# Layer norms given out in small steps, their stores issued from POOL, and the last sums shared by two engines, in a two-layer float32 encoder

## The chip, the cores and the metric

The kernel runs on one core of one Trainium2 chip. The metric is the time of one execution in microseconds on the device; three runs are compared by their median. A profile of one execution shows each engine (PE is TensorE, DVE VectorE, ACT ScalarE, POOL GpSimd, SP SyncE, whose queue issues most DMAs), instruction by instruction. PEclk is the share of its full clock that TensorE was granted.

## The reference

An encoder trunk of two layers runs over two token streams, one of 1024 and one of 256 tokens, each with 16 learned tokens put in front (1040 and 272 positions of 1024 channels, float32). Cut to what matters here:

```python
for i in range(2):
    m = hyena_mixer(h, ...) if i == 0 else attention_mixer(h, ...)
    h = layer_norm(ALPHA * h + m, ln1_g[i], ln1_b[i])
    g, a = jnp.split(h @ ffn_w_in[i], 2, axis=-1)        # 2 x 2816 channels
    f = (gelu(dwconv3(g, conv_w, conv_b)) * a) @ ffn_w_out[i]
    h = layer_norm(ALPHA * h + f, ln2_g[i], ln2_b[i])
return h[:, 16:]

def layer_norm(x, g, b):
    xc = x - mean(x, channels)
    return xc * rsqrt(mean(xc * xc, channels) + 1e-5) * g + b
```

The change is in the second layer norm of each layer, the one behind the product with `ffn_w_out`.

## The kernel before

**Layout.** Channels lie on the 128 partitions in 8 blocks, tokens along the free axis. The tokens of both streams are put into two pairs of chunks: pair p = 0 has two chunks of 384 tokens, pair p = 1 has two of n1 tokens (272 in layer 0; 258 in layer 1, where 14 positions that are not returned are left out). The two chunks of a pair are called c = 0 and c = 1.

**Products.** Each float32 operand is split into a rounded part and a remainder: a cast by ACT (line 259) and a subtraction by DVE (line 260). Each product is three matmuls (lines 288 to 290).

**`ffn_out`** (line 1009) computes the product with `ffn_w_out`. It works in two halves: c = 0 holds the first half of the tokens (chunk 0 of both pairs, up to 656 columns, kept in 8 tiles C), c = 1 the second. Within a half it goes through groups of channel blocks: two groups of four blocks for c = 0; three groups, of 3, 3 and 2 blocks, for c = 1. In a group it goes through the 22 blocks of the inner dimension. Each such step loads a piece of the weight (`raw`, line 1022) and a piece of the hidden values (`hraw`, line 1026) by SP's queue and splits both (`w`, `hq`); up to three steps are prepared ahead (list `ready`), with 4 buffers for `raw`, 3 for `hraw` and 8 each for `w` and `hq` (two to a step). The first two and the last two steps of a group go together (`cuts`). At the last one the residual is loaded into C (line 1054), and DVE adds the product out of PSUM (line 1062) and sums the channel blocks per token into `sms` (line 769).

**The norms as background work.** When a half is done, its two norms (p = 0 and p = 1) are put into a list of generators, `bg`. Each yields the time, in microseconds, after which its next piece is due. After each channel block `ffn_out` calls

```python
                        self.tick(0.9 * (k1 - k0))
```

which takes that time off each generator's count and issues the next piece of those that are due. So the norms of c = 0 are issued between the products of c = 1. Those of c = 1 are issued between the next layer's query, key and value products (layer 0), or at the end by `drain`, which steps the generators in turn, the last one first (layer 1).

**`layer_norm`** (line 771) has these pieces: the mean by a matmul with a constant matrix (line 781); for each of 8 blocks, in two pieces of four, a subtraction (DVE, line 786), a square (ACT, line 788), and the addition of the square into `sm` (POOL, line 790); then the variance by small matmuls (line 796) and the reciprocal root (lines 820 to 825, on ACT and DVE in turn); then the spread of it over the partitions by matmuls (line 804), and for each block, again four and four, a scaling (DVE, line 809), an addition of the bias (ACT, line 810) and `done(f)`. The first matmuls of the mean, the variance and the spread are kept in program order on TensorE. All other instructions are ordered by a scheduler at build time, engine by engine, by program order and its own estimate of when each could run.

**`done`** is `to_x` in layer 0: it splits the block into the operands `y` for the next products and stores it to the buffer `x2d` (line 1403). In layer 1 it is `to_y`, which stores the block to the output (line 1411). Both store by SP's queue, the queue that also loads `raw` and `hraw`. PSUM's tag `ln` (2 banks) holds the mean, the variance and the spread of both norms. The tiles `tp` (9 buffers) hold sums and squares.

`layer_norm` is also used by `window_norms`, for the first norm of each layer.

Of the kernel before, what the change touches and what calls it, by code (L numbers as in the profile page):

```python
# [12 lines left out]
ALU = mybir.AluOpType  # L13
# [65 lines left out]
LAYERS = (Layout(0, 272), Layout(T0, 258))  # L79
# [168 lines left out]
class Trunk:  # L248
# [519 lines left out]
        if f:  # L768
            self.nc.vector.tensor_tensor(out=sm, in0=A[0] if f == 1 else sm, in1=A[f], op=ALU.add)

    def layer_norm(self, A, sm, idx, done):


        nc = self.nc
        v = nc.vector
        n = sm.shape[-1]
        b = self.lnp[:, idx + 1]
        ps = lambda: self.pps.tile([128, 512], F32, tag="ln", name=self.n("ln"), bufs=2)[:, :n]
        mu = ps()
        pin = self.tc.keep_in_program_order  # L780
        pin(nc.tensor.matmul(out=mu, lhsT=self.o1024, rhs=sm, start=True, stop=True))
        nb = -(-n // 128)
        m = 2 * -(-n // (2 * nb))
        at = [min(m * i, n - m) for i in range(nb)]
        for f in range(KC):
            v.tensor_tensor(out=A[f], in0=A[f], in1=mu, op=ALU.subtract)
            sq = sm if f == 0 else self.tp(n)
            nc.scalar.activation(out=sq, in_=A[f], func=AF.Square)  # L788
            if f:
                nc.gpsimd.tensor_tensor(out=sm, in0=sm, in1=sq, op=ALU.add)  # L790
            if f == 3:
                yield 1.5
        yield 8
        var = ps()
        for i, o in enumerate(at):
            x = nc.tensor.matmul(out=var[:m, i:i + 1], lhsT=sm[:, o:o + m], rhs=self.o1024[:, 0:1], start=True, stop=True)
            if i == 0:
                pin(x)
        small = lambda: self.tmp.tile([128, 4], F32, tag="rs", name=self.n("rs"), bufs=6)[:m, :nb]
        r = self.rsqrt(small, var[:m, :nb], nb, self.eps[:m, 0:1], LN_EPS)  # L800
        yield 1.5
        rb = ps()
        for i, o in enumerate(at):
            x = nc.tensor.matmul(out=rb[:, o:o + m], lhsT=r[:, i:i + 1].to_broadcast([m, 128]), rhs=self.ident[:m, :m],
                                 start=True, stop=True)
            if i == 0:
                pin(x)
        for f in range(KC):
            v.scalar_tensor_tensor(out=A[f], in0=A[f], scalar=self.lng2[:, idx, f:f + 1], in1=rb, op0=ALU.mult, op1=ALU.mult)
            nc.scalar.activation(out=A[f], in_=A[f], func=AF.Identity, bias=b[:, f:f + 1])  # L810
            done(f)
            if f == 3:
                yield 3

    def rsqrt(self, t, var, n, eps, epsv, out=None):
# [193 lines left out]
    def ffn_out(self, l, idx, done):  # L1009


        nc = self.nc
        v = nc.vector
        lay, w = LAYERS[l], self.a["w_fout"][l]
        N2 = lay.N2
        half = 2 * -(-N2 // 4)
        sides = ((0, half), (half, N2))

        def load(c, m0, m1, kp):
            cols = (m1 - m0) * 128  # L1020
            r = self.wk.tile([128, 512], F32, tag="raw", name=self.n("raw"), bufs=4)[:, :cols]
            nc.sync.dma_start(out=r, in_=w[kp, :, m0 * 128:m1 * 128])
            wh, wl = (self.wk.tile([128, 512], F32R, tag="w", name=self.n("w"), bufs=8)[:, :cols] for _ in range(2))
            self.split(r, wh, wl)
            r = self.dn.tile([128, 656], F32, tag="hraw", name=self.n("hraw"), bufs=3)[:, :N2]
            nc.sync.dma_start(out=r, in_=self.hd[l][c, kp, :, :N2])
            hh, hl = (self.dn.tile([128, 656], F32R, tag="hq", name=self.n("hq"), bufs=8)[:, :N2] for _ in range(2))
            self.split(r, hh, hl)
            return wh, wl, hh, hl

        groups = ([(0, 0, 4), (0, 4, 8)], [(1, 0, 3), (1, 3, 6), (1, 6, 8)])
        steps = [(*g, kp) for c in range(2) for g in groups[c] for kp in range(MF)]
        cuts = (0, 2) + tuple(range(3, MF - 1)) + (MF,)
        ready = []

        def unit():
            while len(ready) < 3 and steps:
                ready.append(load(*steps.pop(0)))
            return ready.pop(0)

        for c in range(2):
            C = [(self.dn, self.cb)[c].tile([128, 656], F32, tag="c", name=self.n("C"), bufs=8) for _ in range(KC)]
            sms = [self.tp(n) for n in lay.n]
            for _, m0, m1 in groups[c]:
                ps = {}
                for k0, k1 in zip(cuts, cuts[1:]):
                    us = [unit() for _ in range(k0, k1)]
                    for m in range(m0, m1):
                        q = slice(128 * (m - m0), 128 * (m - m0) + 128)
                        A = C[m]  # L1050
                        if k1 == MF:
                            for p in range(2):
                                o = lay.start[p][c]
                                nc.sync.dma_start(out=A[:, 384 * p:384 * p + lay.n[p]], in_=self.xd[l][:, m, o:o + lay.n[p]])
                        for i, (a, b) in enumerate(sides):
                            if k0 == 0:
                                tag, bufs = ("mm", 6) if m - m0 < 3 else ("ln", 2)
                                ps[m, i] = self.pps.tile([128, 512], F32, tag=tag, name=self.n("mm"), bufs=bufs)[:, :b - a]
                            self.mm3(ps[m, i], [(wh[:, q], wl[:, q], hh[:, a:b], hl[:, a:b]) for wh, wl, hh, hl in us],
                                     k0 == 0, k1 == MF)  # L1060
                            if k1 == MF:
                                v.scalar_tensor_tensor(out=A[:, a:b], in0=A[:, a:b], scalar=ALPHA, in1=ps[m, i],
                                                       op0=ALU.mult, op1=ALU.add)
                        if k1 == MF:
                            for p in range(2):
                                self.add_up(sms[p], [z[:, 384 * p:384 * p + lay.n[p]] for z in C], m)
                        self.tick(0.9 * (k1 - k0))
            for p in range(2):
                A = [z[:, 384 * p:384 * p + lay.n[p]] for z in C]
                self.later(("x", 2 * p + c), self.layer_norm(A, sms[p], idx, done(p, c, A)))  # L1070


    def qkv(self, common, later):
# [320 lines left out]
        o = lay.start[p][c] - 1 + d[p and c]  # L1394
        return x[:, m, o:o + lay.n[p] + 2]

    def to_x(self, p, c, A):
        lay = LAYERS[0]
        o, n, at = lay.start[p][c], lay.n[p], c * lay.n[p]

        def f(k):
            self.split(A[k], self.x[p][0][k][:, at:at + n], self.x[p][1][k][:, at:at + n])
            self.nc.sync.dma_start(out=self.x2d[:, k, o:o + n], in_=A[k])
        return f

    def to_y(self, p, c, A):
        s = p and c
        o = LAYERS[1].start[p][c] - LAYERS[1].col(s, T0)

        def f(k):  # L1410
            self.nc.sync.dma_start(out=self.a[f"y_{s}"][:, k, o:o + LAYERS[1].n[p]], in_=A[k])
        return f


# [18 lines left out]
```

## Time and profile before

| | |
|---|---|
| median of 3 runs | 3626.16 us (3624.95 to 3626.39) |
| profiled execution, its time | 3623.7 us |
| span of the profile | 3621.5 us |
| mean granted clock of TensorE | 0.973 |
| DMA moved | 391.69 MB, 108 GB/s |
| DMAs issued by POOL (software queue) | 23.07 MB |

The page of the profile names groups of instructions by line, engine and tile, with their count, busy time and the idle time before them. A view by windows gives the busy time of each engine in a stretch of the execution, with the number of instructions in brackets, the granted clock, the mean busy share of the 16 DMA engines and what they moved. A timeline row gives start, duration, engine, line, operation, tiles, shapes and count, and in square brackets how long the engine was idle before and what it waited for. A row may merge instructions of one line; the shape shown is that of the first.

### The profile page before, as it was taken

Reading aid. Unit: us, or ns where it says so; the run is one execution under the profiler, and the core shown is the slowest. Engines: PE = TensorE matmul, PEld = TensorE weight load, DVE = VectorE, ACT = ScalarE, POOL = GpSimd, SP = SyncE. Lnnn points to the kernel's source line nnn. Section 1 sums busy time; section 2 is a strip of 40 time slices with the busy share of each in tenths; the row PEclk is TensorE's granted clock in tenths of the full one; section 3 lists DMA queues with packets and bytes.
Section 4 is the critical chain, followed back from the end, with each engine's and each line's share of the span. In section 5 each row is a group of like instructions: output and inputs, shape, how many; then the busy total and the mean of one; then the engine's idle time right before and its main releaser. Section 6 shows DMA issues by size and latency. Waiting matters only on the chain.

```text
span 3621.5 us, 61578 instructions
## 1 busy us (share of the span) xinstructions
PE 3425.1 (95%) x23000; PEld 3315.7 (92%) x23000; DVE 2290.0 (63%) x4624; ACT 1707.8 (47%) x3614; POOL 509.0 (14%) x626
## 2 busy tenths in 40 slices
PE   8999999999989999999899999999979999999986
PEld 7999999998879999999898988888979999999986
DVE  6555554664797666654667557776598666654645
ACT  4333333663465444433545447776375444433434
POOL 2434341110110000000102341110110000000101
PEclk8999999999989999999999999999989999999998
DMA  6222223544222212255565440001233222246575
GB/s 169 89 96 91 92 89 114 146 136 139 94 87 92 74 61 75 67 178 178 158 195 166 135 130 16 16 12 44 92 102 97 77 68 66 74 135 203 139 196 139
DMA packets 239741, 391.69 MB, mean 108 GB/s; under 512 B 30580, under 2 KB 134235, under 8 KB 239059
## 3 DMA queue, kind: packets, MB, share of 16 engines
q1 hardware_dynamic: 232659, 364.70, 33.4%
q0 software_dynamic: 6784, 23.07, 1.7%
q8 instruction: 180, 2.95, 0.3%
q14 instruction: 118, 0.97, 0.1%
HBM read 302.22 MB, written 78.84 MB: 105 GB/s over the span
## 4 chain that ended last, share of the span: by engine, by line
PE 63%; DVE 5%; ACT 4%; DMA 2%; POOL 1%; issue 1%; SPq 0%; POOLq 0%; ACTq 0%; DVEq 0%
PE mm L288 17%; PE mm L290 17%; PE mm L289 17%; PE pt L1263 2%; PE sc L288 1%; PE pv L1279 1%; PE pv L1280 1%; DVE w L260 1%; PE pv L1281 1%; PE sc L290 1%; PE sc L289 1%; POOL tp L790 1%; DVE T L260 1%; DMA hraw<-hd 1%; ACT C L810 1%
## 5 line engine op out<-in xcount | busy, mean ns | idle before, releaser
L288 PE MATMUL mm<-T,w 128*128 128x386 f32 (+2 forms) x2464 | 778.0, 316 | 34.4 <-ACT w L259 26.7
L260 DVE TENSOR_TENSOR w<-raw,w 128x512 fp32r<-128x512 f32 (+2 forms) x744 | 511.9, 691 | 437.8 <-ACT w L259 424.3
L259 ACT CAST w<-raw 128x512 fp32r<-128x512 f32 (+2 forms) x744 | 439.1, 593 | 729.2 <-PE mm L289 571.8
L290 PE MATMUL mm<-T,w 128*128 128x386 f32 (+2 forms) x2464 | 774.7, 315 | 3.7 <-DVE w L260 3.4
L289 PE MATMUL mm<-T,w 128*128 128x386 f32 (+2 forms) x2464 | 774.6, 314 | 0.0
L288 PE MATMUL mm<-y,w 128*128 128x386 f32 (+6 forms) x1664 | 543.9, 327 | 14.3 <-ACT y L259 10.2
L290 PE MATMUL mm<-y,w 128*128 128x386 f32 (+6 forms) x1664 | 531.1, 320 | 12.9 <-DVE w L260 12.8
L289 PE MATMUL mm<-y,w 128*128 128x386 f32 (+6 forms) x1664 | 532.5, 320 | 2.6 <-DVE y L260 1.2
L288 PEld LDWEIGHTS mm<-T,w 128*128 128x128 f32 x2464 | 468.3, 190 | 41.9 <-ACT w L259 31.1
L290 PEld LDWEIGHTS mm<-T,w 128*128 128x128 f32 x2464 | 467.7, 190 | 7.8 <-DVE w L260 7.5
L289 PEld LDWEIGHTS mm<-T,w 128*128 128x128 f32 x2464 | 468.9, 190 | 0.3
L288 PE MATMUL mm<-hq,w 128*128 128x328 f32 (+2 forms) x1408 | 440.7, 317 | 23.6 <-ACT hq L259 23.4
L289 PE MATMUL mm<-hq,w 128*128 128x328 f32 (+2 forms) x1408 | 444.3, 316 | 7.0 <-DVE hq L260 7.0
L290 PE MATMUL mm<-hq,w 128*128 128x328 f32 (+2 forms) x1408 | 443.5, 315 | 0.0
L790 POOL TENSOR_TENSOR tp<-tp,tp 128x384 f32<-128x384 f32 (+5 forms) x112 | 116.7, 1050 | 1836.3 <-ACT tp L788 1830.2
L288 PEld LDWEIGHTS mm<-y,w 128*128 128x128 f32 x1664 | 321.3, 193 | 19.0 <-ACT y L259 12.9
L290 PEld LDWEIGHTS mm<-y,w 128*128 128x128 f32 x1664 | 321.5, 193 | 14.8 <-DVE w L260 14.3
L289 PEld LDWEIGHTS mm<-y,w 128*128 128x128 f32 x1664 | 321.3, 193 | 8.2 <-DVE y L260 3.9
L288 PEld LDWEIGHTS mm<-hq,w 128*128 128x128 f32 x1408 | 268.6, 192 | 25.0 <-ACT hq L259 24.9
L289 PEld LDWEIGHTS mm<-hq,w 128*128 128x128 f32 x1408 | 270.5, 192 | 8.8 <-DVE hq L260 8.5
L290 PEld LDWEIGHTS mm<-hq,w 128*128 128x128 f32 x1408 | 270.0, 192 | 0.0
L260 DVE TENSOR_TENSOR hq<-hraw,hq 128x656 fp32r<-128x656 f32 (+1 forms) x220 | 187.1, 851 | 62.4 <-ACT hq L259 58.2
(210 smaller groups left out, 5759.5 us busy)
## 6 DMA issues: line engine op xcount, KB each, us to landing
raw<-in_w_fin SPq DMA_DIRECT2D x208, 256.0 KB
hraw<-hd SPq DMA_DIRECT2D x110, 328.0 KB
hraw<-hd SPq DMA_DIRECT2D x110, 321.0 KB
raw<-in_w_fout SPq DMA_DIRECT2D x88, 256.0 KB
hd<-g SPq DMA_DIRECT2D x88, 192.0 KB
raw<-in_w_fout SPq DMA_DIRECT2D x88, 192.0 KB
raw<-in_w_hin SPq DMA_DIRECT2D x48, 256.0 KB
kk<-kd SPq DMA_DIRECT2D x64, 192.0 KB
```

Of the source, the lines that this page charges most:

```text
L259: self.nc.scalar.copy(out=h, in_=src)
L260: (self.nc.gpsimd if pool else self.nc.vector).tensor_tensor(out=l, in0=src, in1=h, op=ALU.subtract)
L288: mm(out=ps, lhsT=wh, rhs=xh, start=start and i == 0, stop=False, **skip)
L289: mm(out=ps, lhsT=wh, rhs=xl, start=False, stop=False, **skip)
L290: mm(out=ps, lhsT=wl, rhs=xh, start=False, stop=stop and i == last, **skip)
L790: nc.gpsimd.tensor_tensor(out=sm, in0=sm, in1=sq, op=ALU.add)
L810: nc.scalar.activation(out=A[f], in_=A[f], func=AF.Identity, bias=b[:, f:f + 1])
L1263: nc.tensor.transpose(pt[:kn, q0:q0 + m], pr[:m, 128 * j:128 * j + kn], self.ident[:m, :m])
L1279: mm(out=pv, lhsT=vh, rhs=ph[:kn, :nn], start=(jj == 0), stop=False)
L1280: mm(out=pv, lhsT=vh, rhs=pl[:kn, :nn], start=False, stop=False)
L1281: mm(out=pv, lhsT=vl, rhs=ph[:kn, :nn], start=False, stop=last)
```

## The change

`layer_norm` gets two arguments. With `pace` it yields after every block, in both loops, so that a piece is one block instead of four; the waits before the variance and before the spread grow by 6 and 3 us. With `adder` the squares are added by that engine instead of POOL. `ffn_out` passes a pace of 3 us for the norms of c = 0, in both layers, and DVE as adder for the norm of p = 1, c = 1 in layer 1. `done` gets the engine that issues its store: POOL for c = 0, SP for c = 1.

```diff
-    def layer_norm(self, A, sm, idx, done):
+    def layer_norm(self, A, sm, idx, done, pace=0, adder=None):
...
             nc.scalar.activation(out=sq, in_=A[f], func=AF.Square)
             if f:
-                nc.gpsimd.tensor_tensor(out=sm, in0=sm, in1=sq, op=ALU.add)
-            if f == 3:
+                (adder or nc.gpsimd).tensor_tensor(out=sm, in0=sm, in1=sq, op=ALU.add)
+            if pace:
+                yield pace
+            elif f == 3:
                 yield 1.5
-        yield 8
+        yield 8 + 2 * pace
         var = ps()
...
-        yield 1.5
+        yield 1.5 + pace
         rb = ps()
...
             done(f)
-            if f == 3:
+            if pace:
+                yield pace
+            elif f == 3:
                 yield 3
...
+            last = c == l == 1
             for p in range(2):
                 A = [z[:, 384 * p:384 * p + lay.n[p]] for z in C]
-                self.later(("x", 2 * p + c), self.layer_norm(A, sms[p], idx, done(p, c, A)))
+                e = nc.sync if c else nc.gpsimd
+                self.later(("x", 2 * p + c), self.layer_norm(A, sms[p], idx, done(p, c, A, e), 0 if c else 3,
+                                                             v if last and p else None))
...
-    def to_x(self, p, c, A):
+    def to_x(self, p, c, A, e):
...
-            self.nc.sync.dma_start(out=self.x2d[:, k, o:o + n], in_=A[k])
+            e.dma_start(out=self.x2d[:, k, o:o + n], in_=A[k])
...
-    def to_y(self, p, c, A):
+    def to_y(self, p, c, A, e):
...
-            self.nc.sync.dma_start(out=self.a[f"y_{s}"][:, k, o:o + LAYERS[1].n[p]], in_=A[k])
+            e.dma_start(out=self.a[f"y_{s}"][:, k, o:o + LAYERS[1].n[p]], in_=A[k])
```

## The prediction

> **What bounds the kernel now.** I read the page first, then busy time by stage, then the timeline of each engine where the stages differ, then the tail.
>
> ```profile
> span 3621.5 us, 61578 instructions
> PE 3425.1 (95%) x23000; PEld 3315.7 (92%) x23000; DVE 2290.0 (63%) x4624; ACT 1707.8 (47%) x3614; POOL 509.0 (14%) x626
> PE 63%; DVE 5%; ACT 4%; DMA 2%; POOL 1%; issue 1%; SPq 0%; POOLq 0%; ACTq 0%; DVEq 0%
> ```
>
> TensorE (PE) is the bound: what can be won is the time in which it stands still. The change touches only `ffn_out`'s layer norms, so I compare the two halves of `ffn_out` in each layer. Both halves issue the same 1056 products (8 row blocks x 22 steps x 6).
>
> ```profile
> core 0: us, PE busy (x) PEld busy (x) DVE busy (x) ACT busy (x) POOL busy (x), PEclk, DMA share, GB/s
> 1592.80:1753.70 160.90, 160.81 (x1056) 160.29 (x1057) 75.89 (x114) 55.10 (x88) 0.00 (x0) 0.99 0.64 201
> 1753.70:1934.80 181.10, 168.22 (x1087) 166.54 (x1086) 122.66 (x216) 93.56 (x184) 15.58 (x15) 0.95 0.65 195
> 3236.00:3396.30 160.30, 160.06 (x1056) 159.97 (x1057) 74.74 (x114) 54.79 (x89) 0.00 (x0) 0.98 0.65 199
> 3396.30:3583.50 187.20, 166.71 (x1086) 164.77 (x1084) 113.20 (x198) 85.42 (x165) 15.11 (x14) 0.95 0.68 177
> 3583.50:3621.50 38.00, 6.82 (x29) 5.62 (x28) 16.44 (x42) 14.76 (x36) 11.96 (x14) 0.55 0.32 69
> ```
>
> Rows one to four are layer 0 first half, layer 0 second half, layer 1 first half, layer 1 second half; row five is the tail. Beside the same products, a second half holds the first half's two layer norms, and it takes 20.2 us (layer 0) and 26.9 us (layer 1) longer. Where those go, layer 0 first (timelines of POOL, PE, SP's queue, DVE):
>
> ```profile
> 1758.20 6.59 DVE L786 TENSOR_TENSOR C<-C,ln 128x384 f32<-128x384 f32 x16 [0.16 <-PE ln L781]
> 1759.86 16.21 POOL L790 TENSOR_TENSOR tp<-tp,tp 128x384 f32<-128x384 f32 x14 [721.30 <-ACT tp L788]
> 1771.63 1.44 PE L796 MATMUL ln<-squares,tp 128*128 128x1 f32 x6 [2.92 <-POOL tp L790]
> 1776.12 1.08 PE L796 MATMUL ln<-squares,tp 128*92 128x1 f32 x6 [3.06 <-POOL tp L790]
> 1785.27 13.15 SPq L1403 DMA_DIRECT2D x2d<-C  x16
> 1798.61 0.64 PE L289 MATMUL mm<-hq,w 128*128 128x328 f32 x1 [6.31 <-DVE hq L260]
> ```
>
> The 16 subtractions come in one burst. POOL needs 16.2 us for the 14 sums of squares behind it, and TensorE, whose variance products stand in its order, waits for POOL twice. Then the 16 scalings with their splits come in a burst, and their 16 stores hold SP's queue for 13.2 us, with the loads of the next operands behind them: TensorE runs dry for 6.3 us. Layer 1 (the second row is the first load after the stores):
>
> ```profile
> 3424.96 0.33 SPq L1022 DMA_DIRECT2D raw<-in_w_fout  x1
> 3427.22 15.97 SPq L1411 DMA_DIRECT2D y<-C  x16
> 3443.28 3.10 SPq L1026 DMA_DIRECT2D hraw<-hd  x2
> 3413.98 0.83 PE L796 MATMUL ln<-squares,tp 128*128 128x1 f32 x6 [2.93 <-POOL tp L790]
> 3418.34 1.04 PE L796 MATMUL ln<-squares,tp 128*86 128x1 f32 x6 [3.52 <-POOL tp L790]
> 3454.77 0.73 ACT L259 CAST hq<-hraw 128x642 fp32r<-128x642 f32 x1 [17.16 <-DMA hraw<-hd]
> 3455.55 0.64 PE L288 MATMUL mm<-hq,w 128*128 128x322 f32 x1 [13.81 <-ACT hq L259]
> 3450.00:3455.00 5.00, 0.00 (x0) 0.00 (x0) 0.00 (x0) 0.23 (x1) 0.00 (x0) 0.50 0.84 137
> 3428.40:3450.00 21.60, 13.34 (x87) 12.67 (x85) 9.31 (x19) 9.21 (x20) 0.00 (x0) 0.93 1.05 137
> ```
>
> Same picture, larger: no load is issued from 3425 to 3443, and the loads behind the stores land only near 3454.7. TensorE stands 13.8 us and restarts at half clock. In the last row (columns as in the stages) the DMA engines are full (share 1.05) at 137 GB/s while the stores go out.
>
> **The change, part by part.**
>
> *Pace (both layers, first half only).* Each of the 8 subtraction steps, the wait for the sum, the reciprocal root and the 8 scaling steps becomes its own step, due 3 us of ticks after the one before. Ticks are 0.9 us for six products (1.8 where two operand steps go together), so a step comes every 3.6 us, for both norms at once. From the code: first step 3.6 us after the half begins, last subtraction at 28.8, variance at 46.8, scalings from about 52 to 77 of some 158 us. So they end inside the half, and nothing later waits for them.
>
> What can be had: floor of a second half = first half, less its own cold start (clock 0.99 and 0.98: 1.6 and 3.2 us, which I take as 2.4 for each), plus the norms' own matmuls. The latter are two mean groups (1.27 us, taken from the row of the same operation below), and four variance and spread groups of about 0.83 to 1.04 us: 4.6 us in all. Floor 163.1 and 162.5; stalls now 181.1 - 163.1 = **18.0** and 187.2 - 162.5 = **24.7 us**.
>
> ```profile
> 1938.99 1.27 PE L781 MATMUL ln<-tp,squares 128*128 128x384 f32 x4
> 1820.00:1830.00 10.00, 10.00 (x69) 10.00 (x68) 4.86 (x8) 4.40 (x8) 0.00 (x0) 1.00 0.68 194
> 1830.00:1840.00 10.00, 10.00 (x68) 10.00 (x67) 7.74 (x16) 2.97 (x7) 0.00 (x0) 1.00 0.45 137
> 1784.00:1801.00 17.00, 14.55 (x32) 13.54 (x32) 0.82 0.55 189
> L790 POOL TENSOR_TENSOR tp<-tp,tp x28: 756/1021/1611, 1759.9 to 1955.7; 128x384 f32<-128x384 f32 x14, 128x272 f32<-128x272 f32 x14
> 1925.54 0.32 SPq L1026 DMA_DIRECT2D hraw<-hd  x1
> 1934.77 0.34 PE L288 MATMUL mm<-y,w 128*128 128x384 f32 x1
> L467 POOL DMA_DIRECT2D kd<-ko x56: 539/552/599, 122.9 to 565.3; - x56
> ```
>
> *POOL wait.* POOL's sums: two per 3.6 us at about 1.0 us each (fifth row) is 2 us of work in 3.6. The variance comes 18 us after the last step, so both variance waits go (about 6 us a layer, and the slow clock after them). Next late is the spread matmul: it is due 4.5 us after the variance and needs the chain ACT, DVE, ACT, DVE, DVE of the reciprocal root between other work. I charge **1 us** a layer for it.
>
> *DVE in layer 0.* The fourth row is the work on tile C in the burst (DVE, then ACT): 14.55 us of DVE for the 16 scalings and 16 splits. Spread over 25.2 us (7 intervals of 3.6) they add 0.58 to the 0.49 that DVE has in a plain stretch (second row): 1.07. The change from the first to the second group of row blocks falls into that time (54 to 65 us of ticks) and adds 2.9 us in a ten-microsecond window (third row less second) and about half of that beside it, 4 to 5 in all. Demand 14.6 + 12.3 + 4.8 = 31.7 us in 25.2, so DVE falls behind by up to 6.5 us. Cover: operands are split two to three steps ahead (2.7 us each), 5 to 8 us. Loss between 0 and 6; I take **3 us**, in the middle, since the rows' busy times overlap somewhat. Layer 1 has no splits here: half the DVE work, no loss.
>
> *Stores to POOL's queue.* 16 stores a layer leave SP's queue, so the loads are no longer held: this is worth layer 1's 13.8 us and layer 0's 6.3 us. On POOL an issue costs about 0.55 us (last row, POOL's own DMAs earlier): 16 x 0.55 = 9 us a layer on an engine that has nothing else then; what waits behind a waiting store there is only the next store. The bytes remain: in layer 1 the stores are 8 x (384 + 258) columns x 128 rows x 4 bytes = 2.63 MB, at 137 GB/s 19 us of full DMA engines. In the 8 x 3.6 = 28.8 us of the scalings the loads need 0.68 of the engines, 20 us, and the residuals for the group's end about 3 (1 MB at 200 GB/s for a share of 0.68): 42 in 28.8, 13 us late. Cover: loads run ahead. In layer 1 TensorE ran on until 3441.7 (3455.55 less 13.81) after the last load at 3425, 17 us; at layer 0's end the last load is issued 9.2 us before the products are over. Loss 0 to 4 if the loads get their part, all 13.8 us if they don't; I take **3 us**.
>
> *Last sums on two engines (layer 1, tail).* Rows of the tail:
>
> ```profile
> 3585.93 6.47 DVE L786 TENSOR_TENSOR C<-C,ln 128x258 f32<-128x258 f32 x16 [0.86 <-PE ln L781]
> 3587.28 9.53 POOL L790 TENSOR_TENSOR tp<-tp,tp 128x258 f32<-128x258 f32 x11 [169.00 <-ACT tp L788]
> 3597.80 3.13 POOL L790 TENSOR_TENSOR tp<-tp,tp 128x384 f32<-128x384 f32 x3 [0.99 <-ACT tp L788]
> 3600.98 1.44 PE L796 MATMUL ln<-squares,tp 128*128 128x1 f32 x6 [4.04 <-POOL tp L790]
> L769 DVE TENSOR_TENSOR tp<-tp,C x3: 421/422/559, 3582.9 to 3584.7; 128x258 f32<-128x258 f32 x2, 128x384 f32<-128x384 f32 x1
> ```
>
> POOL's 14 sums end at 3600.9 and release the last variance. After the change POOL has the 7 of 384 columns, 1.04 us each; DVE adds 7 of 258 columns, 0.42 us each (last row). DVE then has 6.5 + 2.9 = 9.4 us and is done near 3595.3. POOL does three sums by 3593, waits for the second four subtractions (done near 3594), and adds four: 3598.3. Gain **2.7 us**. Bounds: POOL without a pause from 3589.1, 3596.4 (gain 4.6); if DVE waits a whole ACT step, about 0.9 us, before each of its sums, a loss of 2.
>
> Sum against the profiled execution (3623.7 us; its span of 3621.5 and 2.2 around it): 18.0 - 4 = 14.0, 24.7 - 4 = 20.7, tail 2.7: 37.4 us, 3586.3. The median of the runs is 2.5 us above the profiled one: **3589 us**.
>
> The Trainium skill, "TensorE: Matmul & The Clock Gate" (Part 1), says an idle time of about 3.4 us puts the clock to one half until a similar time of activity has passed. The trace agrees with the second half of it (0.50 after the 13.8 us gap, row 3450). By that rule each of my two remaining losses, if it is one piece of 4 us, would cost an estimated 1.7 us more: 3592 instead of 3589.
>
> **Rivals.**
>
> *The loads still wait (layer 1).* The stores are as many bytes on the same DMA engines, full at 137 GB/s already (row 3428.40). If loads get their share only after the stores, 12 of the 13.8 us and the slow restart stay: 3589 + 13 = 3602. For it: share 1.05. Against it: the loads then stood behind the stores in one queue, and stores now come at the rate of the scalings. The Trainium skill, "DMA: Bandwidth & Descriptors" (Issuing engines are not separate DMA queues), says just this: a second issuing engine saves only the issue time. No row here shows two queues under load together.
>
> *DVE is the bound of layer 0's scalings.* If the whole 6.5 us and more (waits of ACT and DVE on each other in each step) reach TensorE and the group's change costs layer 1 as well: 6 + 4 us back, 3599.
>
> *Everything fits.* No loss of 4 + 4, tail gain 4.6: 3589 - 10 = 3579.
>
> *Slower.* Each paced step makes DVE and ACT wait for each other in order, with the next operands' splits behind them. There are 32 such steps in the two layers, and 18.0 + 24.7 + 2.7 = 45 us to be had; so it decides from 1.4 us of stopped TensorE a step. At the 1.6 us that ACT idles for the first scaling of a burst (row below) it would be 32 x 1.6 = 51 us, 3632. Against it: the lead is refilled between steps, DVE being half idle.
>
> ```profile
> 1784.63 1.14 ACT L810 ACTIVATE C<-C,lnp 128x384 f32<-128x384 f32 x2 [1.61 <-DVE C L809]
> ```
>
> *No effect.* The stalls are conserved: the same work returns as small waits that add to 45 us less what the tail gives. Nothing in the rows asks for it.
>
> **How the numbers follow.** Forecast 45%, loads still wait 20%, DVE bound 14%, everything fits 12%, slower 5%, no effect 4%. Differences under 0.2% (7 us) can't be told from none. Faster: 0.91; same 0.04; slower 0.05. The range takes in the first four cases with their bounds: 3577 to 3605.
>
> **What would show it.** Right: the second halves near 167 us each with clock 0.98 or more; no wait of the variance products for POOL; no DMA wait of ACT beyond 3 us in layer 1; sums on POOL in seven plus seven small pieces; the last variance near 3598. Wrong: a dry TensorE at the change of groups in layer 0 (about 62 us into the half), or at 52 to 80 us into layer 1's half with the DMA share above 1.

## The result, and the profile after

| | before | after |
|---|---|---|
| median | 3625.55 us (4 runs, 3622.19 to 3626.39) | 3579.87 us (4 runs, 3577.93 to 3584.23) |
| profiled execution | 3623.7 us, span 3621.5 | 3577.93 us, span 3575.6 |
| mean granted clock of TensorE | 0.973 | 0.978 |

The changed kernel takes 0.9877 of the time (95% interval 0.986 to 0.9894): 45.7 us less. Runs of one kernel differ by some 6 us, so a single total tells little here; a stage of the profile tells more.

The changed kernel's page: the busy time of each engine, and the shares of the chain that ended last.

```profile
span 3575.6 us, 61608 instructions
PE 3415.6 (96%) x23000; PEld 3307.6 (93%) x23000; DVE 2296.8 (64%) x4631; ACT 1708.4 (48%) x3614; POOL 523.8 (15%) x651
PE 63%; DVE 6%; ACT 3%; DMA 3%; issue 1%; POOL 0%; SPq 0%; POOLq 0%; ACTq 0%; DVEq 0%
```

Of the chain, POOL's 1% has gone. The view by windows of the changed kernel, in the five stages of the prediction (layer 0 first and second half of `ffn_out`, layer 1 first and second half, tail); the columns are the same:

```profile
1589.15:1751.20 162.05, 161.67 (x1057) 161.16 (x1058) 75.93 (x114) 55.15 (x88) 0.00 (x0) 0.98 0.63 200
1751.20:1914.15 162.95, 162.85 (x1086) 161.96 (x1085) 122.98 (x216) 93.95 (x184) 25.80 (x31) 1.00 0.70 216
3217.50:3377.80 160.30, 160.25 (x1056) 159.78 (x1057) 74.75 (x114) 54.59 (x88) 0.00 (x0) 0.98 0.63 199
3377.80:3539.70 161.90, 161.77 (x1086) 160.66 (x1084) 113.88 (x198) 85.24 (x165) 25.61 (x30) 1.00 0.72 205
3539.70:3575.60 35.90, 6.71 (x29) 5.62 (x28) 19.95 (x49) 15.03 (x36) 7.27 (x7) 0.57 0.35 74
```

TensorE is busy for all but 0.1 us of each second half, at full clock. Layer 0's second half went from 181.10 to 162.95 us (18.15 less), layer 1's from 187.20 to 161.90 (25.3 less), the tail from 38.0 to 35.9 (2.1 less). The stages that the change does not touch give 0.35 us together (3.65 less before the first row, 1.15 more in it, 2.15 more between the layers). The sum is 45.9, which is 3621.5 - 3575.6.

When the pieces of layer 0's norms ran in the changed kernel (view of one line: min/median/max in ns, then first and last start):

```profile
L786 DVE TENSOR_TENSOR C<-C,ln x16: 423/486/557, 1755.6 to 1771.8; 128x384 f32<-128x384 f32 x8, 128x272 f32<-128x272 f32 x8
L798 PE MATMUL ln<-squares,tp x12: 166/220/250, 1799.2 to 1800.2; 128*128 128x1 f32 x6, 128*92 128x1 f32 x6
L811 DVE SCALAR_TENSOR_TENSOR C<-C,lng,ln x16: 484/548/609, 1806.9 to 1833.8; 128x384 f32<-128x384 f32 x8, 128x272 f32<-128x272 f32 x8
```

The variance comes 48 us into the half and nothing waits for it. The scalings are spread over 27 us. The subtractions are spread over only 16: the build-time scheduler drew them ahead of their due times, so POOL still works almost without a pause, but it has until 1799 to finish.

### The profile page after: what moved, and what is told of

The parts are those of the page before. It is cut to its first block, busy times and chain, and to the rows that moved or that the text cites. A ratio compares the mean times of both kernels' runs of the same rounds, so it can differ in the third digit from the quotient of the medians.

```text
span 3575.6 us, 61608 instructions
## 1 busy us (share of the span) xinstructions
PE 3415.6 (96%) x23000; PEld 3307.6 (93%) x23000; DVE 2296.8 (64%) x4631; ACT 1708.4 (48%) x3614; POOL 523.8 (15%) x651
## 4 chain that ended last, share of the span: by engine, by line
PE 63%; DVE 6%; ACT 3%; DMA 3%; issue 1%; POOL 0%; SPq 0%; POOLq 0%; ACTq 0%; DVEq 0%
PE mm L288 17%; PE mm L290 17%; PE mm L289 17%; PE pt L1270 2%; DMA hraw<-hd 1%; PE sc L288 1%; DVE w L260 1%; PE pv L1286 1%; PE pv L1287 1%; PE pv L1288 1%; PE sc L289 1%; PE sc L290 1%; DVE T L260 1%; PE rs L1277 1%; DMA raw<-in_w_fin 1%
## 5 line engine op out<-in xcount | busy, mean ns | idle before, releaser
L790 POOL TENSOR_TENSOR tp<-tp,tp 128x384 f32<-128x384 f32 (+4 forms) x105 | 115.3, 1110 | 1753.7 <-ACT tp L788 1749.2
```

What stands on the lines that cost most here:

```text
L790: (adder or nc.gpsimd).tensor_tensor(out=sm, in0=sm, in1=sq, op=ALU.add)
```

## The experiments

Each changes the kernel after, unless it says otherwise. For each I give the median, the ratio to the kernel before in the same job (95% interval), and the two second halves and the tail of its profiled execution. To compare with: 181.1, 187.2 and 38.0 us before; 163.0, 161.9 and 35.9 after. First the parts of the change one at a time, then the limits of what covers the work, then the tail.

**Pace alone.** Stores stay on SP's queue, all sums on POOL.

```diff
-                e = nc.sync if c else nc.gpsimd
+                e = nc.sync
...
-                                                             v if last and p else None))
+                                                             None))
```

> Steps paced by 3 us as in the changed kernel; the stores of the first half go out by SP's queue again, and POOL does all last sums. Theory A (each part of the change takes away its own wait, and SP's queue is the larger one): the variance waits are gone in both layers, but the loads still stand behind the stores in SP's queue; second half of layer 0 near 168 us, of layer 1 near 176 us, time near 3600 us. Theory B (spacing alone is enough: a store that waits holds the loads for less than the lead of the loads): both second halves within 3 us of the changed kernel's 163.0 and 161.9 us, time 3580 to 3586 us, no gap of TensorE over 2 us in these halves.

Measured: 3581.6 us (3574.69 to 3586.91), ratio 0.9876 (0.9857 to 0.9895); 162.9, 161.1 and 37.8. Its two second halves by windows, then a stretch of SP's queue in layer 1:

```profile
1747.67:1910.54 162.87, 162.59 (x1086) 161.97 (x1085) 122.94 (x216) 94.34 (x184) 17.16 (x15) 1.00 0.72 216
3373.58:3534.64 161.06, 161.06 (x1086) 160.63 (x1084) 113.95 (x198) 85.37 (x165) 17.02 (x14) 1.00 0.73 206
3430.20 1.55 SPq L1418 DMA_DIRECT2D y<-C  x3
3432.25 0.34 SPq L1026 DMA_DIRECT2D raw<-in_w_fout  x1
3432.69 1.77 SPq L1418 DMA_DIRECT2D y<-C  x3
3434.55 0.40 SPq L1030 DMA_DIRECT2D hraw<-hd  x1
```

The whole gain of the halves is there without POOL's queue. Paced, stores and loads alternate on SP, and a load waits for some 1.8 us of store issues, not for 16.

**POOL's queue alone.** Bursts as before, stores of the first half from POOL.

```diff
-    ... done(p, c, A, e), 0 if c else 3,
-                                                             v if last and p else None))
+    ... done(p, c, A, e), 0,
+                                                             None))
```

> Bursts of four blocks as in the kernel before; only the stores of the first half go out by POOL's queue; POOL does all last sums. Theory A: the wait for loads is gone (13.8 us in layer 1, 6.3 us in layer 0, with the slow restart), the two variance waits stay (about 6 us a layer and the slow clock after them); second halves near 173 and 172 us, time near 3602 us. Theory B: the bursts themselves hold the splits, so the second halves stay above 176 us and the time above 3608 us.

Measured: 3621.21 us (10 runs), ratio 0.9986 (0.9975 to 0.9997); 180.7, 182.0 and 38.7. Its timeline of PE and SP's queue, the windows row of tile C in layer 0 (DVE, ACT, POOL), and layer 1's gap on PE:

```profile
1769.08 1.39 PE L798 MATMUL ln<-squares,tp 128*128 128x1 f32 x6 [2.89 <-POOL tp L790]
1780.85 0.33 SPq L1026 DMA_DIRECT2D raw<-in_w_fout  x1
1796.48 0.33 SPq L1030 DMA_DIRECT2D hraw<-hd  x1
1796.47 0.64 PE L289 MATMUL mm<-hq,w 128*128 128x328 f32 x1 [6.31 <-DVE hq L260]
1781.50:1795.50 14.00, 13.53 (x30) 12.69 (x31) 7.76 (x15) 0.91 0.49 176
3448.99 0.64 PE L288 MATMUL mm<-hq,w 128*128 128x322 f32 x1 [5.55 <-ACT hq L259]
```

In layer 0 the gap is 6.31 us, what it was before, though no store is on SP's queue. The loads still pause from 1780.85 to 1796.48, because their buffers are not free: DVE works on the norms for 13.53 of 14 us, and the splits that would free the buffers stand behind (SP's longest wait in this stretch is 15.3 us, for DVE's split of `hq`). In layer 1 the gap falls from 13.81 to 5.55 us; there the queue is worth 5 us of half. The waits of the variance stay.

**The longer wait alone.** Bursts, SP's queue and POOL's sums as before; only the wait before the variance of the first half grows, from 8 to 20 us of ticks. The cut is against the kernel before.

```diff
-        yield 8
+        yield 8 + 4 * pace
```

> As the kernel before (pieces of four blocks, stores by SP's queue, POOL's sums), only the wait between the last square and the variance of the first half's norms grows from 8 to 20 us. Theory (the variance waits cost their 6 us a layer and the slow clock behind them, and nothing else): these gaps go, the later gaps of 6.3 and 13.8 us stay; second halves 171 to 174 us and 177 to 180 us, time 3606 to 3612 us. Rival (the burst of subtractions and POOL's sums that slow DVE hold the operands as well): gaps of 2 us or more come in the place of the variance waits; halves 176 us and more and 182 us and more, time over 3614 us.

Measured: 3608.88 us (3605.75 to 3609.79), ratio 0.9951 (0.9934 to 0.9967); 173.5, 179.2 and 39.0. Its timeline of PE, what is left:

```profile
1802.79 0.64 PE L289 MATMUL mm<-hq,w 128*128 128x328 f32 x1 [5.62 <-DVE hq L260]
3453.80 0.64 PE L288 MATMUL mm<-hq,w 128*128 128x322 f32 x1 [12.89 <-ACT hq L259]
```

The two variance waits of each layer go, and the halves lose 7.6 and 8.0 us: 6.0 and 6.5 of them are the waits themselves, 0.7 and 0.9 a shorter gap at the scalings. Those gaps stay otherwise. So some 15.6 of the 43.4 us that the halves gave come from this one wait, without another queue and without small pieces.

**DVE's sums alone.** `adder` without the rest.

```diff
-                e = nc.sync if c else nc.gpsimd
+                e = nc.sync
-    ... done(p, c, A, e), 0 if c else 3,
+    ... done(p, c, A, e), 0,
```

> Only the last norm of pair 1 in layer 1 adds its squares on DVE; no pace, all stores by SP's queue. Theory (tail gains 2 to 3 us, nothing else moves): tail after the last product near 35.9 us as in the changed kernel against 38.0 before, time 3622 to 3625 us, not to be told from before by time alone. Rival (the tail's gain came from something else, such as the stores): tail near 38 us.

Measured: 3623.01 us (10 runs), ratio 0.9991 (0.9982 to 1.0001); 181.1, 186.8 and 36.6. Its tail by windows:

```profile
3586.08:3622.70 36.62, 6.85 (x30) 5.62 (x28) 20.10 (x49) 15.03 (x36) 7.29 (x7) 0.59 0.33 73
```

The tail gives 1.4 us, too little to be seen in the total.

**Pieces without the small steps.** Pieces of four blocks as before, but 14 us apart.

```diff
-            if pace:
-                yield pace
-            elif f == 3:
-                yield 1.5
-        yield 8 + 2 * pace
+            if f == 3:
+                yield 14 if pace else 1.5
+        yield 8 + 3 * pace
...
-            if pace:
-                yield pace
-            elif f == 3:
-                yield 3
+            if f == 3:
+                yield 14 if pace else 3
```

> As the changed kernel, but a piece is again four blocks at once, and the waits between pieces are those of four single steps (14.4 us of ticks), so the norms end at the same place as in the changed kernel. Theory A (single blocks matter: a burst of four with its splits holds the operands longer than they were prepared ahead): a gap of 3 us or more in at least one second half; halves 167 to 172 us, time 3586 to 3600 us. Theory B (it is the time between the pieces that matters, above all that the sum is done before the variance is due): halves within 2 us of 163.0 and 161.7 us, time 3577 to 3584 us.

Measured: 3589.16 us (3584.73 to 3597.11), ratio 0.9899 (0.9883 to 0.9915); 164.8, 168.3 and 37.5. Its largest gap on PE in each layer:

```profile
1816.49 0.42 PE L288 MATMUL mm<-hq,w 128*128 128x328 f32 x1 [1.29 <-DVE C L1062]
3442.11 0.64 PE L288 MATMUL mm<-hq,w 128*128 128x322 f32 x1 [4.54 <-ACT hq L259]
```

In layer 0 the time between bursts does nearly all; in layer 1 the half is still 6.4 us longer than after: behind a burst of eight stores ACT waits 9.1 us for a load, and TensorE 4.54 us for ACT.

**A shorter pace.** 1 us instead of 3.

```diff
-    ... done(p, c, A, e), 0 if c else 3,
+    ... done(p, c, A, e), 0 if c else 1,
```

> As the changed kernel, with a pace of 1 us instead of 3: a step every 1.8 us of ticks, and shorter waits before the variance (10 us) and the spread (2.5 us). Theory A (the lead of the loads and splits, some 17 and 5 to 8 us, is what covers the steps): at double rate DVE falls some 14 us behind in layer 0 and the loads some 17 us in layer 1, beyond the lead; second halves 168 to 173 us, time 3588 to 3600 us. Theory B (any spacing finer than the bursts will do): second halves within 2 us of the changed kernel's, time 3577 to 3584 us.

Measured: 3587.51 us (3583.05 to 3592.8), ratio 0.9894 (0.9875 to 0.9913); 163.0, 168.9 and 37.1. Five microseconds of layer 0 by windows, layer 1's half, and a cast and a product of layer 1 in its timeline:

```profile
1790.00:1795.00 5.00, 5.00 (x35) 5.00 (x35) 5.00 (x12) 5.00 (x13) 2.03 (x5) 1.00 0.91 249
3374.85:3543.73 168.88, 164.72 (x1086) 162.43 (x1084) 113.67 (x198) 85.53 (x165) 25.94 (x30) 0.98 0.71 197
3434.68 0.73 ACT L259 CAST hq<-hraw 128x642 fp32r<-128x642 f32 x1 [4.24 <-DMA hraw<-hd]
3435.46 0.64 PE L288 MATMUL mm<-hq,w 128*128 128x322 f32 x1 [2.62 <-ACT hq L259]
```

Layer 0 loses nothing with DVE and ACT both full and TensorE beside them, against the expected 14 us of lateness. At this pace the scalings run from 35 to 53 us into the half and are over when the change of groups (61 to 65 us in this trace) adds its work. Layer 1 loses 7 us, and the chain there is load, cast, product.

**The shorter pace, without the bytes.** As the last one, with the first half's output stores of layer 1 left out.

```diff
-            e.dma_start(out=self.a[f"y_{s}"][:, k, o:o + LAYERS[1].n[p]], in_=A[k])
+            if c:
+                e.dma_start(out=self.a[f"y_{s}"][:, k, o:o + LAYERS[1].n[p]], in_=A[k])
```

> As the run with a pace of 1 us, but in layer 1 the stores of the first half are left out (that half of the output is not written). That run lost 6.9 us in layer 1's second half (168.9 us), with ACT waiting for loads, and nothing in layer 0 (163.0 us). Theory (the DMA engines, full with the stores to the output, bring the loads late): second half of layer 1 161 to 163 us, no gap of TensorE over 1 us there. Rival (the double rate of DVE's and ACT's steps delays the splits): it stays above 167 us.

Measured: one run, 3586.61 us; 163.4, 161.7 and 36.2. Layer 1's half by windows:

```profile
3386.79:3548.51 161.72, 161.57 (x1086) 160.66 (x1084) 113.97 (x198) 85.06 (x165) 17.30 (x14) 1.00 0.64 189
```

The 7 us are gone (168.88 to 161.72; the DMA share falls from 0.71 to 0.64). So in layer 1 it is the stores' bytes on the DMA engines that delay the loads. The total is no lower because other stages of this one execution were longer than in the run before: 7.8 us ahead of layer 0's `ffn_out`, 3.4 between the layers. Why is not known.

**A shorter lead.** Two steps prepared ahead instead of three, with the buffers to match.

```diff
-            ... tag="hraw", name=self.n("hraw"), bufs=3)[:, :N2]
+            ... tag="hraw", name=self.n("hraw"), bufs=2)[:, :N2]
...
-            ... tag="hq", name=self.n("hq"), bufs=8)[:, :N2] for _ in range(2))
+            ... tag="hq", name=self.n("hq"), bufs=6)[:, :N2] for _ in range(2))
...
-            while len(ready) < 3 and steps:
+            while len(ready) < 2 and steps:
```

> As the changed kernel, but operands are prepared one step less ahead: two instead of three steps in the list, 6 instead of 8 buffers for hq, 2 instead of 3 for hraw. Theory (what hides the paced norms is the lead of splits and loads): the first halves, without norms, stay at 160 to 162 us, the second halves get gaps and grow to 167 us or more in layer 1 (loads late by the stores) and 165 us or more in layer 0 (DVE late). Rival (the engines have time enough between paced steps, so the lead is not used): second halves within 2 us of 163.0 and 161.7 us.

Measured: 3618.61 us (9 runs), ratio 0.9983 (0.9973 to 0.9992); 178.7, 182.6 and 37.4, with first halves of 161.6 and 160.25 as after. The first 118 us of layer 1's second half, the stretch that holds the norms, by windows: here, then in the kernel after.

```profile
3391.99:3510.00 118.01, 111.22 (x725) 108.51 (x725) 75.30 (x131) 60.04 (x116) 24.72 (x30) 0.99 0.72 193
```

```profile
3377.81:3495.80 117.99, 117.92 (x795) 117.33 (x794) 82.82 (x141) 64.39 (x125) 25.61 (x30) 1.00 0.76 211
```

Beside the norms it issues 70 products fewer in the same time, at 0.15 us each 10.4 us late (118 us for 795). The first halves lose nothing by the shorter lead. 1 us of it is lost 21 us into the half, the rest between 68 and 97 us, while the last stores go out, and nothing in the 20 us of the same group behind them. So in layer 1 the lead of loads is what covers the paced norms. The other half of the 20.7 us is lost in the last group of two blocks, where no norm runs: there the shorter lead hurts by itself. In layer 0 that is most of it: of 15.7 us only 3.7 are lost beside the norms, 12 in the last group.

**All of layer 0's norms paced.** Also those of its second half, which run in the next layer's query, key and value products.

```diff
-    ... done(p, c, A, e), 0 if c else 3,
+    ... done(p, c, A, e), 0 if c and l else 3,
```

> As the changed kernel, and in layer 0 the norms of the second half, which are issued between the next layer's query, key and value products, are paced by 3 us as well (their stores stay in SP's queue). In the changed kernel TensorE stands 8.5 us in gaps between 14 and 63 us after that half. Theory (the same cure): these gaps go but for 2 us, and some slow clock with them; time 3570 to 3575 us. Rival (these products have chains of their own over ACT, POOL and DVE, and the gaps are theirs): gaps stay, time 3577 to 3583 us.

Measured: 3588.82 us (3586.25 to 3589.77), ratio 0.9894 (0.988 to 0.9909); 162.3, 164.2 and 36.8. The waits of TensorE there got fewer (gaps over 0.4 us: 1.80, 1.46, 0.74 and 1.29, where the kernel after has at least seven), yet the time did not fall. 114 us behind that half TensorE is 1.7 us ahead of the kernel after; by 190 us it is 3.6 us behind, in part by waits of 0.32, 1.21, 1.33 and 1.59 us for DVE (after: 0.57, 0.37 and 1.05). The stage between the layers ends 5.1 us longer, so the waits moved and did not go. What moved them is not settled. Layer 1's second half, which this edit leaves alone, is 2.3 us longer than after's; see the residuals below.

**The sums of squares on DVE.** For both layers, but for the last norm.

```diff
-                                                             v if last and p else None))
+                                                             None if c and not (last and p) else v))
```

> As the changed kernel, but the squares of the first half's norms are added by DVE instead of POOL, in both layers. In the changed kernel DVE's subtractions for the operands (0.56 us for w, 0.84 us for hq) take 1.1 and 1.2 to 1.7 us while POOL adds. Theory (POOL and DVE slow each other when both take two inputs from SBUF): with POOL idle all these subtractions are back at 0.56 and 0.84 us, DVE's busy time in the second halves is no larger than 123 and 114 us although it does 14 sums more; halves 162 to 164 us, time 3577 to 3584 us. Rival (the longer durations are waits for ACT's casts, counted as busy): they stay long, and DVE's busy time grows by 6 us.

Measured: 3582.41 us (3575.14 to 3585.73), ratio 0.9878 (0.9861 to 0.9894); 162.7, 165.1 and 36.7. Layer 0's half by windows and one split in its timeline; then the same split in the kernel after.

```profile
1753.34:1916.03 162.69, 162.58 (x1086) 161.96 (x1085) 122.51 (x230) 94.22 (x184) 8.82 (x17) 1.00 0.72 216
1766.81 0.83 DVE L260 TENSOR_TENSOR hq<-hraw,hq 128x656 fp32r<-128x656 f32 x1
```

```profile
1766.30 1.68 DVE L260 TENSOR_TENSOR hq<-hraw,hq 128x656 fp32r<-128x656 f32 x1
```

In layer 0 DVE does 14 sums more (x230 against x216) in 0.5 us less (122.51 against 122.98), since its other instructions no longer run beside POOL's sums; in layer 1 it does 14 more in 0.6 us more (114.52 against 113.88). Layer 1's half is 3.2 us longer than after's: 86 us into it TensorE waits 1.53 us for ACT, which has waited 3.95 us for a load. Two runs that leave this half alone show the same (see the residuals below), so it need not come from the sums. The total is that of the kernel after within the error.

**The tail in another order.** The last drain steps p = 0 first.

```diff
-                            self.drain()
+                            while self.bg:
+                                for e in list(self.bg):
+                                    self.step(e)
```

> As the changed kernel, but at the end the two last norms are stepped with pair 0 first, whose squares POOL adds, instead of pair 1 first. Theory (POOL's seven sums, 7.7 us, start with the first squares and no longer wait for pair 1's subtractions): POOL starts about 2 us earlier, the last variance comes 3 to 4 us earlier, the tail is 32 to 34 us instead of 36.0, time 3575 to 3579 us. Rival (DVE, with 9.4 us of subtractions and sums, ends no earlier, so pair 1's variance takes the place of pair 0's): tail 35 to 37 us.

Measured: 3581.87 us (3576.73 to 3582.62), ratio 0.9873 (0.9856 to 0.9889); 162.7, 161.1 and 36.3. The last variance on PE:

```profile
3558.19 1.04 PE L798 MATMUL ln<-squares,tp 128*86 128x1 f32 x6 [1.59 <-DVE tp L790]
```

POOL is done sooner, but now DVE's sums end last: the variance starts 15.3 us after the last product, as in the kernel after (15.4). The wait changed hands.

**One set of squares added by TensorE.** That order, and the squares of p = 1 go into PSUM by small matmuls, with no addition by DVE or POOL.

```diff
...
+            if pe:
+                for i, o in enumerate(at):
+                    pin(nc.tensor.matmul(out=var[:m, i:i + 1], lhsT=sq[:, o:o + m], rhs=self.o1024[:, 0:1],
+                                         start=f == i == 0, stop=f == KC - 1, skip_group_check=True))
-            if f:
+            elif f:
...
-                                                             v if last and p else None))
+                                                             nc.tensor if last and p else None))
...
```

> As the changed kernel, but at the end pair 0's norm is stepped first, and pair 1's squares are added by TensorE (small matmuls that add into the variance in PSUM) instead of DVE. Theory (DVE and POOL slow each other in the tail, so neither of their shares can shrink while both add): without DVE's sums POOL's seven additions take 1.0 us each from about 2 us after the first subtraction, the last variance is out 12 us after the last product instead of 15.4, and the tail is 32 to 34 us instead of 36.0; time 3574 to 3579 us. Rival (TensorE, at half clock, needs 1.04 us for each of eight groups and becomes the late one, or pair 0's additions end no earlier): tail 35.5 us or more, time as the changed kernel's.

Measured: 3579.76 us (3577.43 to 3583.64), ratio 0.9875 (0.9859 to 0.9891); 163.4, 164.0 and 34.8. POOL's sums and the tail by windows:

```profile
3547.32 7.45 POOL L796 TENSOR_TENSOR tp<-tp,tp 128x384 f32<-128x384 f32 x7 [81.34 <-ACT tp L790]
3543.25:3578.10 34.85, 12.48 (x72) 11.31 (x70) 16.35 (x42) 14.64 (x36) 6.98 (x7) 0.58 0.41 76
```

POOL adds its seven without a pause, and the last variance starts 12.0 us after the last product instead of 15.4. The tail gets only 1.1 us shorter, and the total cannot be told from that of the kernel after. No version here clearly beats it.

## Why the prediction was right, and where it was not

**The stalls: right.** 18.0 and 24.7 us were to be had; 18.15 and 25.3 were had. The floor worked out from the first halves (163.1 and 162.5) is where the second halves ended (162.95 and 161.9). The sum took all stalls as gone, whichever part of the change takes them; so it came out although the parts were credited wrongly, as the next points say.

**The residuals: mis-sized.** I left 1 + 3 us in layer 0 and 1 + 3 in layer 1; in the profiled execution all four measured nothing. So the halves gave 8.75 us more than forecast. The tail gave 0.6 less and the untouched stages 0.35 more, which makes the 8.5 by which the sum fell short (37.4 against 45.9). So the rival "Everything fits" gave the time, 3579, though its tail did not come. What happened in place of each:

- The spread matmul (1 us a layer): neither second half has a gap on PE above 0.25 us.
- DVE in layer 0 (3 us): DVE is as full as I said, but TensorE never runs out. Two stretches of the kernel after by windows:

```profile
1810.00:1815.00 5.00, 5.00 (x35) 5.00 (x34) 5.00 (x13) 4.12 (x10) 1.62 (x3) 1.00 0.68 224
1820.00:1825.00 5.00, 5.00 (x36) 5.00 (x35) 5.00 (x10) 4.50 (x10) 1.38 (x3) 1.00 0.97 310
```

- DMA in layer 1 (3 us): the engines are as full as I said, and in this execution the lead covers it. The stores' time and its fullest piece by windows, and ACT's waits for loads in that half (total, times, longest), in the kernel after:

```profile
3434.70:3465.00 30.30, 30.23 (x204) 29.97 (x203) 22.69 (x43) 18.07 (x36) 8.63 (x16) 1.00 0.95 217
3440.00:3445.00 5.00, 5.00 (x36) 5.00 (x35) 5.00 (x11) 2.70 (x5) 0.54 (x1) 1.00 1.15 151
ACT hq L259 <- DMA hraw<-hd: 23.1, 20, 3.9
```

ACT waits up to 3.9 us for a load, more than the 3 I named as the sign of a loss, and TensorE is busy for 30.23 of 30.30 us. The sign was the wrong one: a wait of ACT costs nothing while split operands lie ready. But here the lead only just suffices. Three runs leave this half alone, with the same instructions in the same order on DVE, ACT, POOL and SP: the tail in another order (161.1 us), all of layer 0's norms paced (164.2) and the squares added by TensorE (164.0). In the second of them, 85 us into the half:

```profile
3467.80 0.73 ACT L259 CAST hq<-hraw 128x642 fp32r<-128x642 f32 x1 [3.84 <-DMA hraw<-hd]
3468.58 0.41 PE L288 MATMUL mm<-hq,w 128*128 128x322 f32 x1 [0.88 <-ACT hq L259]
```

A wait of ACT as long as after's now stops TensorE. So this term lay between 0 and some 2.3 us from one execution to the next, and the 25.3 us of layer 1 are the good end.

Both terms could have been seen from the prediction's own rows. I had a lateness of up to 6.5 us against a cover of 5 to 8, and of 13 us against a cover of 17 (TensorE ran on for 17 us after the last load), and charged the middle all the same. The shorter lead shows that this cover is what holds in layer 1; the pace of 1 us shows where it ends there. In layer 0 only the bursts 14 us apart come near its end (a gap of 1.29 us, for DVE).

**Stores to POOL's queue: the wrong reason.** I credited the queue with "layer 1's 13.8 us and layer 0's 6.3 us". With the queue alone layer 0's gap stayed at 6.31, and layer 1's half got 5 us shorter; with the pace alone both went on SP's queue too. In layer 0, SP's 13 us of stores stood beside a burst that fills DVE (13.5 of 14 us in the run with POOL's queue alone); the row of PE named DVE as the releaser, and I read past it. In layer 1 the queue is a part of it, 5 us; that the stores' bytes delay the loads as well is shown at the pace of 1 us, with and without the stores. So the rival "The loads still wait" had the right resource and the wrong outcome: spread at one step per 3.6 us, the bytes fit, or nearly. The Trainium skill, "DMA: Bandwidth & Descriptors" (Issuing engines are not separate DMA queues), says that a second issuing engine saves only the time of the issue; the trace agrees, POOL's queue being worth 5 us where 16 issues hold up SP (layer 1), and nothing measurable once they are paced (0.9876 against 0.9877). It may even cost: with paced stores on SP's queue ACT's longest wait for a load in layer 1's half was 1.9 us, in five traces with them on POOL's 3.3 to 5.2. The former is one trace, so this is not shown.

**The pace before the variance: right, by another way.** The variance did come 48 us into the half (46.8 forecast) and its waits went. But the sums are not the "two per 3.6 us" that I forecast: they run in 19 us, and the longer wait alone was enough to save 15.6 us.

**The tail: 2.1 us, not 2.7.** The last variance started 15.4 us after the last product instead of 14.8. The sums in the tail of the kernel after:

```profile
3545.75 3.21 POOL L790 TENSOR_TENSOR tp<-tp,tp 128x384 f32<-128x384 f32 x3 [82.51 <-ACT tp L788]
3550.47 4.46 POOL L790 TENSOR_TENSOR tp<-tp,tp 128x384 f32<-128x384 f32 x4 [1.51 <-ACT tp L788]
3554.98 1.44 PE L798 MATMUL ln<-squares,tp 128*128 128x1 f32 x6 [3.04 <-POOL tp L790]
L790 DVE TENSOR_TENSOR tp<-tp,tp 128x258 f32<-128x258 f32 x7 | 3.8, 549 | 0.0
```

POOL began its last four 10.8 us after the last product (10.5 forecast) and took 4.46 us (4.16 forecast); DVE's seven sums took 3.8 us, not 2.9. The tail also differs between executions: in the eight traces where DVE adds these squares and the order is after's it takes 35.9 to 37.5 us (mean 36.8), in the four where POOL adds all of them 37.8 to 39.0 (mean 38.4). So the change is worth about 1.6 us there, and the 2.1 are the good end.

**The clock.** Row 3450 of the prediction lies inside the gap of 13.8 us, not behind it (no instruction of PE is in it). In layer 0 the granted clock was 0.50 from 1772 to 1781 of the kernel before, at two waits of 2.92 and 3.06 us, shorter than the idle time by which the prediction gets its 3592. Nothing hung on it, as no such wait was left in the second halves.

## What to carry to other kernels

In these runs, work beside the bound engine cost nothing until its lateness exceeded the lead of what that engine eats. Put the lateness and the lead in microseconds side by side, and charge only what stands over; full side engines and their waits alone are no loss. Where the two are near each other, expect the loss in some executions, and look at more than one trace. Where a gap has two causes beside it (a queue held by stores, a burst on DVE), start from the releaser that the row names, and look for the plain wait first: giving POOL time before the variance was a third of the gain and needed one number.

## What the runs showed of the hardware that I had not expected

DVE's instructions with two inputs from SBUF take up to twice as long while POOL adds. DVE's sums in the tail of the kernel after, in its timeline; POOL adds from 3545.75 to 3548.96 and again from 3550.47:

```profile
3544.17 0.42 DVE L790 TENSOR_TENSOR tp<-tp,tp 128x258 f32<-128x258 f32 x1
3547.24 0.87 DVE L790 TENSOR_TENSOR tp<-tp,tp 128x258 f32<-128x258 f32 x1
3548.36 0.88 DVE L790 TENSOR_TENSOR tp<-tp,tp 128x258 f32<-128x258 f32 x1
3549.64 0.42 DVE L790 TENSOR_TENSOR tp<-tp,tp 128x258 f32<-128x258 f32 x1
```

The same sum takes 0.42 us alone and 0.87 beside POOL; a split takes 0.83 and up to 1.68, and goes back to 0.83 where POOL's sums are taken away. The subtractions of the mean, whose second input lies in PSUM, keep their 0.42 to 0.56 us beside POOL's sums (row L786 of the kernel after). The Trainium skill, "SBUF — State Buffer" (Who interferes with whom), has the rule: an instruction of DVE with two SBUF inputs contends with one of GpSimd that reads SBUF. The trace agrees. Offloading to POOL is therefore not free for DVE: here what DVE saved by the 14 sums on POOL was given back by its slower rest.
